# Latent attention's rotated keys on all 128 rows, with zeros in the other head's half

## The chip, the cores and the metric

One core of a Trainium2 chip runs the whole program. The time is device microseconds of one execution; the figure before is the median of three runs.

## What is computed

Two blocks on 256 tokens with 1024 features, all in float32: a retention layer and a latent-attention layer, each with a gated embedding behind it, then a block of convolution, pooling and a feed-forward part. The change concerns the scores of the latent attention, with 16 heads, of which this is the core:

```python
k_rope = rope(z[..., o2:o3][:, :, None, :], pos)[:, :, 0, :]
...
q = (c_q @ w_uq).reshape(B, S, MLA_HEADS, MLA_NOPE + MLA_ROPE)
q_nope = q[..., :MLA_NOPE]
q_rope = rope(q[..., MLA_NOPE:], pos)
q_abs = jnp.einsum('bshd,chd->bshc', q_nope, w_uk)
scale = (MLA_NOPE + MLA_ROPE) ** -0.5
q_cat = jnp.concatenate([q_abs, q_rope], axis=-1) * scale
k_cat = jnp.concatenate([c_kv, k_rope], axis=-1)
...
s = jnp.einsum('bqhc,bkc->bhqk', qb, k_cat).astype(jnp.float32)
s = jnp.where(key_idx[None, :] <= q_idx[:, None], s, neg)
pr = jax.nn.softmax(s, axis=-1).astype(c_kv.dtype)
```

A head's score is a sum of two products: one over 128 features without rotation, and one over 64 rotated features, whose keys all heads share.

## The kernel before

Activations lie transposed, features on the 128 rows and the 256 tokens along the columns. Weights come from DRAM in tiles of 128 x 1024, in the order of their use, through six buffers (`fetch`, L162). Each float32 operand of a product is taken as a sum of two parts, `hi` and `lo`, in the type float32r: ScalarE copies `hi` (L175 for weights, L184 for activations), VectorE subtracts for `lo` (L176, L185). `mm` (L233) then issues three products: hi x hi (L234), hi x lo (L235), lo x hi (L236). The profile calls a weight's parts `wh` and `wl`.

The order on TensorE is the order in which the program is written, with one device: `after(us, fn)` puts `fn` behind about so much emitted TensorE time. ScalarE, VectorE and GpSimd have their own queues, whose order the scheduler decides from the dependences.

In the retention layer, each of four heads multiplies keys with queries (L568), and values with scores (`ret_av`, L585 and L586: two values' blocks to a bank, two banks, each of 256 columns, then 128 more). Its rotary tables are `cosR` and `sinR` (L481, L482), last read at L555 and L556.

In the latent attention the heads go in pairs p = 0 to 7. The 64 rotated key features are computed twice over, so that rows 0 to 63 and rows 64 to 127 hold the same; `rope4` (L737) rotates them and splits them into `krh` and `krl`, once for all heads (L782). `mla_proj` (L823) makes a pair's queries: `qr` holds the rotated queries of head 2p on rows 0 to 63 and of head 2p + 1 on rows 64 to 127; `qn` and `kn` hold the 128 features without rotation. `mla_scores` (L852) takes, for each head e of the pair and each block of 128 queries, first the product over 128 rows (L861), then the one over the head's 64 rows (L862), both into the same sum:

```python
for e in range(2):
    pss = bank()
    rs = slice(64 * e, 64 * e + 64)
    for qb, (o, n) in enumerate(((0, P), (P, S))):
        qs = slice(qb * P, (qb + 1) * P)
        mm(pss[:, o:o + n], (qn[0][:, e, qs], qn[1][:, e, qs]), (kn[0][:, e, :n], kn[1][:, e, :n]), True, False)
        mm(pss[:, o:o + n], (qr[0][rs, qs], qr[1][rs, qs]), (kr[0][rs, :n], kr[1][rs, :n]), False, True)
```

That is 24 products to a pair: per head three of 128 columns on 128 rows, three of 128 on 64 rows, three of 256 on 128 rows, three of 256 on 64 rows. Here these 24 are called a score block; there are eight. Behind a block come the softmax on VectorE and ScalarE (L865 to L878), and on TensorE other work: gates (`mla_gate`, L800, whose product VectorE takes at L809) and the next pair's projections. `mla_turn` transposes the probabilities (L889), `mla_av` (L896) multiplies them with the values. Steps of the modulation (L409), a dot product per partition on VectorE of a tile that a transfer brings, are put between at a set rate.

Of the kernel before, what the change touches and what calls it, by code (L numbers as in the profile page):

```python
# [11 lines left out]
F32 = mybir.dt.float32  # L12
# [70 lines left out]
def tile_kernel(ctx, tc, order, xT, pT, pos, vec, cst, cv, wada, wts, outT):  # L83
# [22 lines left out]
    class Blk:  # L106
        """nb feature blocks of [128, 256], four to a tile."""
        def __init__(self, nb, dt=F32):
# [11 lines left out]
    class Wide(Blk):  # L120
        """eight blocks of 256 + extra columns"""
        def __init__(self, extra):
# [16 lines left out]

# [1 line left out]
    class Seq:  # L141
# [47 lines left out]

    # A start clears the accumulation bits of its whole PSUM bank, so a bank in which two  # L190
    # sums are open together is started once, over all its columns.
    def open_bank():
# [3 lines left out]

    # Emission order is the software pipeline: `after(us, fn)` emits fn once about that much
    # tensor-engine time has been emitted behind it, so that what fn waits for is done by then.
    clk = [0.0]
# [6 lines left out]

    # the modulation's steps on VectorE, one per `rate` of emitted tensor-engine time
    mods = {"rate": None, "last": 0.0, "n": 0}
# [36 lines left out]

# [1 line left out]
    xt = Blk(DB)  # L247
# [5 lines left out]

    # the first products are taken in float32, from the tiles as they come
    v0 = [("ret_in", kb * P, 2048) for kb in range(8)]
# [13 lines left out]
    V.memset(ones, 1.0)  # L269
    # the tensor engine's clock rises only after some microseconds of work: done while it waits  # L270
    wu = bank()
# [16 lines left out]

# [1 line left out]
    def sum_pairs(pairs):  # L290
        """squares of [128, 2, 256] pieces, added up"""
        tot = None
        for i, p in enumerate(pairs):
            sq = t2()
            A.activation(sq, p, AF.Square)
            if tot is None:
                tot = sq
            elif i < len(pairs) - 1:
                V.tensor_add(tot, tot, sq)
        return [tot, sq] if len(pairs) > 1 else [tot]  # L300

    def sum_ahead(pairs):
        """All but the last added up."""
        tot = pairs[0]
        for i, p in enumerate(pairs[1:-1]):
            new = t2() if i == 0 else tot
            V.tensor_add(new, tot, p)
            tot = new
        return [tot] + pairs[1:][-1:]

    def warm(x):
        """has the reciprocal square root's table loaded before it is waited for"""
        A.activation(small(1), x, AF.Abs_reciprocal_sqrt, bias=eps_r)

    class Sums:
        """Sums over the features of pieces [128, n, 256] that come one by one, and of their squares:
        the early pieces are added up, the last ones go to the tensor engine as they are."""
        def __init__(self, both, fold):
# [53 lines left out]
    def rms_neg2(ps, n, out=None):  # L372
        """-2/sqrt(sum/n + eps), on every partition."""
        ve = t1()
        V.tensor_scalar(ve, ps, 1.0 / n, RMS_EPS, MUL, ADD)
        r0 = t1()
        A.activation(r0, ps, AF.Abs_reciprocal_sqrt, bias=eps_r, scale=1.0 / n)
        return newton(r0, ve, t1(tag="nr", bufs=3) if out is None else out)

    def ln_stats(ps, n):  # L380
        """ps: sum, sum of squares -> mean, -2/sqrt(var + eps)."""
        mu = t1(tag="mu", bufs=2)
# [11 lines left out]

# [1 line left out]
    mod = cp.tile([P, 48], F32, name="mod")  # L396
# [22 lines left out]
    def every(us, n, step):  # L419
        """n calls of step, one per us of emitted tensor-engine time."""  # L420
        def run():
# [8 lines left out]

# [1 line left out]
    posf = t1(tag="posf", bufs=1)  # L432
# [29 lines left out]

    # =============== layer 0: retention ===============
    def prenorm(x, layer, then):
        """Split x*g; then(-2*rstd) once the sums are through."""
        pair = two(DB)
# [13 lines left out]

    cosR = cp.tile([P, S], F32, name="cosR")  # L481
    sinR = cp.tile([P, S], F32, name="sinR")  # L482
    rc = cp.tile([P, 2], F32, name="rc")
# [125 lines left out]

    # y = gated @ w_out, K = 2048, eight output tiles kept in four banks  # L610
    def out_proj(name, pairs, ka, rate, done, layer):
# [16 lines left out]
    class proj_banks:  # L628
        """eight tiles of output: three banks of two, and two of one"""
        def __init__(self):  # L630
# [8 lines left out]
        def piece(self, m):  # L639
            """the bank that tile m ends"""  # L640
            return self.b[m // 2] if m < 6 else self.b[m - 3][:, 0:1, :]

    def proj_sums(both, get, key):
        """what to do as tiles end: their sums, without the last two's wait for the others"""
        sums = Sums(both, {"r": 0, "m": 0, "d": 1}[key])
# [17 lines left out]
    def post(x, ys, sums, layer, prepared):  # L663
        """x + rms(y)*g, then the per-layer embedding gate."""
        x1 = Blk(DB)
# [24 lines left out]
    def half_outer(name, xpair, fin, nk=8):  # L690
        """x @ w, eight output tiles: the first four tiles k-outer, the rest n-outer."""
        seq = Seq([(name, kb * P, m * P) for kb in range(nk) for m in range(4)] + nouter(name, range(4, 8), range(nk)))
# [35 lines left out]

    # =============== layer 1: latent attention ===============
    gq = cp.tile([P, 8], F32, name="gq")  # L730
# [3 lines left out]
    krs = t1(tag="krs", bufs=1)  # L734
    kr = (cp.tile([P, S], F32R, name="krh"), cp.tile([P, S], F32R, name="krl"))

    def rope4(src, pair):  # L737
        """rows [x1, x2, x1, x2] x 32 -> rotated, split."""
        sw = t1()
# [5 lines left out]
        V.tensor_add(a, a, sw)  # L745
        split(pair[0], pair[1], a)

# [8 lines left out]
    def lora(banks, sq, n, first):  # L756
        """rms_norm of z = r*zr over n features, from the raw zr."""
        pst = bank()[:, :S]
# [22 lines left out]
    V.scalar_tensor_tensor(krs, pskr, -0.5, r1["nr"], MUL, MUL)  # L781
    rope4(krs, kr)  # L782
    sqkv = sum_pairs([pskv])
# [16 lines left out]
    def mla_gate(p):  # L800
        """silu gates of heads 2p, 2p + 1"""
        if p % 2 == 0:
# [20 lines left out]
    def mla_proj(p):  # L823
# [4 lines left out]
        qr = st["qr"] = (t1(F32R, "qrh", 2), t1(F32R, "qrl", 2))  # L828
        rope4(psr, qr)
        psq = bank2()  # L830
# [21 lines left out]
    def mla_scores(p):  # L852
# [3 lines left out]
        for e in range(2):  # L856
            pss = bank()
            rs = slice(64 * e, 64 * e + 64)
            for qb, (o, n) in enumerate(((0, P), (P, S))):
                qs = slice(qb * P, (qb + 1) * P)  # L860
                mm(pss[:, o:o + n], (qn[0][:, e, qs], qn[1][:, e, qs]), (kn[0][:, e, :n], kn[1][:, e, :n]), True, False)  # L861
                mm(pss[:, o:o + n], (qr[0][rs, qs], qr[1][rs, qs]), (kr[0][rs, :n], kr[1][rs, :n]), False, True)  # L862
            sm = tp.tile([P, 384], F32, tag="am", name=nm("sm"), bufs=2)
# [59 lines left out]

    # =============== block 2 ===============
    # modulation columns: sh1, sc1, g1, sh2, sc2, g2
    while mods["n"] < 41:
# [21 lines left out]
    def modulate(x, which, mu, nrl, pairs, pair, raw=None):  # L948
        """(x - mu) * rstd * (1 + scale) + shift, split."""
        shift = mod[:, 24 * which:24 * which + 8]  # L950
# [15 lines left out]

    # The first four tiles behind a layer norm are multiplied before its statistics are there:
    # the norm is linear in x but for a factor and an offset per token, which are applied to the
    # product, with the column vectors that the offsets need carried as extra moving columns.
    # These products are taken in float32, so that nothing has to be split for them.  # L970
    def ahead(extra):
# [6 lines left out]
    def ahead_mm(name, tiles, w, n, k_outer=4):  # L978
        """the first k_outer tiles side by side, the rest one after the other"""
        first, rest = tiles[:k_outer], tiles[k_outer:]  # L980
# [35 lines left out]
    def ahead_out(ps):  # L1016
        """-> value without its offset, offset column"""
        u = small(2)
# [21 lines left out]

    # one tap of two blocks: on VectorE alone, or with the products from ScalarE
    def conv_steps():
# [49 lines left out]

    # pooling
    # From here most tiles take their product in float32: one more pass, but no splitting on
    # VectorE, which the convolution needs.
    def in_tile(ps, m, parts):
# [175 lines left out]

    # the products of z*g*s with the two norms' factors and offsets put to them
    def up_ahead(i):
# [156 lines left out]
```

## Time and profile before

| | |
|---|---|
| median of three runs | 880.08 us (879.75 to 881.86) |
| span of the profiled execution, its own time on the page | 878.7 us |
| TensorE busy | 862.8 us (98%), 6472 products |
| loads of weights busy | 827.5 us (94%) |
| VectorE busy | 710.7 us (81%) |
| ScalarE busy | 558.0 us (64%) |
| GpSimd busy | 3.2 us |
| mean granted clock of TensorE | 0.989 |

The span runs from the first to the last instruction of one execution; the median of the runs lies 1.4 us above it. Products overlap in the records: one of 256 columns shows some 0.28 us, while the next one starts 0.12 us later. So a stretch of TensorE is read by the starts, not by adding up durations, and a busy share of 98% doesn't say how many products pass. The granted clock is given as a share of 2.4 GHz.

### The profile page before, as it was taken

How to read it: one execution, taken by the hardware profiler on the slowest of the kernel's cores; microseconds unless marked ns; L12 is line 12 of the kernel's file. 1: busy time of each engine (PE TensorE's matmuls, PEld its weight loads, DVE VectorE, ACT ScalarE, POOL GpSimd, SP SyncE). 2: the span in 40 equal slices, each digit the busy share in tenths (PEclk: the TensorE clock that was granted, in tenths of full speed). 3: DMA queues.
4: the chain of work that ended last, by engine and by line, in shares of the span. 5: the costliest groups of instructions: out<-in, count | busy, mean ns of one | idle time of the engine just before them, and what ended most of it. 6: DMA issues, size and time to landing. Idle time of an engine off the chain costs nothing.

```text
span 878.7 us, 16459 instructions
## 1 busy us (share of the span) xinstructions
PE 862.8 (98%) x6472; PEld 827.5 (94%) x6472; DVE 710.7 (81%) x1276; ACT 558.0 (64%) x942; POOL 3.2 (0%) x20
## 2 busy tenths in 40 slices
PE   8999999999999999999999999999999999999994
PEld 6989999999999999999999998999999999999993
DVE  6999778887878977698775578799677888889975
ACT  7666555545675786676554757999756676666533
POOL 0000000000000000000000000000000000000000
PEclk9999999999999999999999999999999999999997
DMA  8857566878466537265245444244464355567601
GB/s 332 320 199 249 186 230 203 280 261 304 147 211 206 229 123 257 103 218 189 98 133 168 169 173 161 99 167 170 144 223 137 132 189 188 188 227 255 204 35 48
DMA packets 46461, 165.95 MB, mean 189 GB/s; under 512 B 5168, under 2 KB 5936, under 8 KB 46384
## 3 DMA queue, kind: packets, MB, share of 16 engines
q1 hardware_dynamic: 46224, 164.39, 54.0%
q8 instruction: 50, 0.82, 0.4%
q0 software_dynamic: 160, 0.52, 0.2%
q14 instruction: 27, 0.22, 0.1%
HBM read 163.85 MB, written 1.05 MB: 188 GB/s over the span
## 4 chain that ended last, share of the span: by engine, by line
PE 97%; DVE 2%; DMA 1%; ACT 0%; SPq 0%; issue 0%
PE ps L234 28%; PE ps L235 27%; PE ps L236 27%; PE ps L240 9%; PE ps L359 2%; PE ps L337 1%; DMA half<-in_xT 1%; PE ps L889 1%; PE ps L194 1%; DVE t L1227 0%; DVE t L1224 0%; PE ps L1145 0%; PE ps L1137 0%; DVE half L676 0%; DVE wl L176 0%
## 5 line engine op out<-in xcount | busy, mean ns | idle before, releaser
L234 PE MATMUL ps<-half,wh 128*128 128x256 f32 x1680 | 476.7, 284 | 0.0
L235 PE MATMUL ps<-half,wh 128*128 128x256 f32 x1680 | 474.6, 283 | 0.1
L236 PE MATMUL ps<-half,wl 128*128 128x256 f32 x1680 | 472.5, 281 | 0.0
L175 ACT CAST wh<-raw 128x1024 fp32r<-128x1024 f32 x233 | 243.1, 1049 | 177.6 <-PE ps L235 132.5
L176 DVE TENSOR_TENSOR wl<-raw,wh 128x1024 fp32r<-128x1024 f32 x233 | 282.2, 1220 | 71.7 <-ACT wh L175 69.6
L235 PEld LDWEIGHTS ps<-half,wh 128*128 128x128 f32 x1680 | 318.1, 189 | 1.6 <-DVE half L185 0.7
L234 PEld LDWEIGHTS ps<-half,wh 128*128 128x128 f32 x1680 | 317.7, 189 | 1.6 <-issue 0.2
L236 PEld LDWEIGHTS ps<-half,wl 128*128 128x128 f32 x1680 | 318.6, 190 | 0.0
L240 PE MATMUL ps<-half,raw 128*128 128x256 f32 (+2 forms) x384 | 84.9, 380 | 0.0
L240 PEld LDWEIGHTS ps<-half,raw 128*128 128x128 f32 x384 | 72.5, 190 | 10.0
L409 DVE CUSTOM_DVE_ANT_0 adach<-adach,siluc 128x1024 f32<-128x1024 f32 x48 | 58.3, 1219 | 19.0 <-DMA adach<-in_wada 18.9
L1054 ACT ACTIVATE t<-apad,vec 128x256 f32<-128x256 f32 x106 | 44.4, 500 | 0.5 <-DVE half L1055 0.5
L1055 DVE TENSOR_TENSOR half<-half,t 128x512 f32<-128x512 f32 x53 | 36.4, 687 | 3.8 <-ACT t L1054 1.8
L184 ACT CAST half<-t 128x256 fp32r<-128x256 f32 (+1 forms) x47 | 20.6, 453 | 21.1 <-DVE t L1317 12.0
L234 PE MATMUL ps<-wh,half 128*128 128x512 f32 (+1 forms) x92 | 33.9, 370 | 0.0
L235 PE MATMUL ps<-wl,half 128*128 128x512 f32 (+1 forms) x92 | 32.7, 356 | 0.2 <-DVE wl L176 0.2
L236 PE MATMUL ps<-wh,half 128*128 128x512 f32 (+1 forms) x92 | 32.6, 355 | 0.0
L185 DVE TENSOR_TENSOR half<-t,half 128x256 fp32r<-128x256 f32 (+1 forms) x47 | 21.7, 483 | 3.7 <-ACT half L184 2.9
L1312 ACT ACTIVATE t<-ps,vec 128x256 f32<-128x256 f32 x38 | 21.0, 557 | 2.7 <-DVE t L1314 1.5
L235 PEld LDWEIGHTS ps<-wl,half 128*128 128x128 f32 x92 | 17.4, 189 | 2.9 <-DVE wl L176 0.6
L234 PEld LDWEIGHTS ps<-wh,half 128*128 128x128 f32 x92 | 17.4, 189 | 2.8 <-ACT wh L175 0.2
L236 PEld LDWEIGHTS ps<-wh,half 128*128 128x128 f32 x92 | 17.3, 188 | 2.6
(260 smaller groups left out, 997.4 us busy)
## 6 DMA issues: line engine op xcount, KB each, us to landing
raw<-in_wts SPq DMA_DIRECT2D x257, 512.0 KB, 4.1
adach<-in_wada SPq DMA_DIRECT2D x48, 512.0 KB, 4.5
half<-in_xT SPq DMA_DIRECT2D x4, 256.0 KB, 6.4
cst<-in_cst SPq DMA_DIRECT2D x1, 928.0 KB, 10.7
raw<-in_wts SPq DMA_DIRECT2D x2, 256.0 KB, 4.9
siluc<-in_cv SPq DMA_DIRECT2D x1, 512.0 KB, 8.8
t<-in_pT POOLq DMA_DIRECT2D x2, 256.0 KB, 4.6
out<-half SPq DMA_DIRECT2D x4, 128.0 KB, 2.0
```

What stands on the lines that cost most here:

```text
L175: A.copy(hi, raw)
L176: V.tensor_sub(lo, raw, hi.bitcast(F32))
L184: A.copy(hi, src)
L185: V.tensor_sub(lo, src, hi.bitcast(F32))
L234: T.matmul(ps, l[0], r[0], start=first, stop=False)
L235: T.matmul(ps, l[0], r[1], start=False, stop=False)
L236: T.matmul(ps, l[1], r[0], start=False, stop=last)
L240: T.matmul(ps, w, r, start=first, stop=last)
L409: V.tensor_tensor_reduce(ch, ch, sc, 1.0, 0.0, MUL, ADD, mod[:, n:n + 1])
L1054: A.activation(t[:, b, :], apad[:, i0 + b, k:k + S], AF.Copy, scale=w[b])
L1055: V.tensor_add(acc.pair(i0 // 2), acc.pair(i0 // 2), t)
L1312: A.activation(t[:, b, :], ps[:, b, :], AF.Identity, bias=col("b_dw_f_2", m), scale=w[2])
```

## The change

The keys are kept in two tiles instead of one, `kr[0]` for the first head of each pair and `kr[1]` for the second, each with both parts. In `kr[e]` the 64 rows of head e hold the rotated keys, the other 64 rows hold zeros. The second product of a score then runs over all 128 rows of `qr` and of `kr[e]`; the other head's queries meet the zeros.

The zeros are written by GpSimd, and the split into parts is done once for each half. `rope4` is given a function that takes the rotated tile, since only the keys are put down in this way; the queries are split as before. The two tiles lie in a pool of two buffers, tag `rot`, in which the retention's rotary tables `cosR` and `sinR` come to lie as well, in one tile.

```diff
-    cosR = cp.tile([P, S], F32, name="cosR")
-    sinR = cp.tile([P, S], F32, name="sinR")
+    rot = tp.tile([P, 2, S], F32, tag="rot", name="rot", bufs=2)
+    cosR, sinR = rot[:, 0, :], rot[:, 1, :]
...
-    kr = (cp.tile([P, S], F32R, name="krh"), cp.tile([P, S], F32R, name="krl"))
+    kr = [tp.tile([P, 2, S], F32R, tag="rot", name=nm("kr"), bufs=2) for _ in range(2)]
...
-    def rope4(src, pair):
+    def rope4(src, put):
...
-        split(pair[0], pair[1], a)
+        put(a)
+
+    def put_kr(a):
+        for e in range(2):
+            own, other = slice(64 * e, 64 * e + 64), slice(64 - 64 * e, 128 - 64 * e)
+            nc.gpsimd.memset(kr[e][other].bitcast(F32), 0.0)
+            split(kr[e][own, 0, :], kr[e][own, 1, :], a[own])
...
-    rope4(krs, kr)
+    rope4(krs, put_kr)
...
-        rope4(psr, qr)
+        rope4(psr, lambda a: split(qr[0], qr[1], a))
...
-            rs = slice(64 * e, 64 * e + 64)
             for qb, (o, n) in enumerate(((0, P), (P, S))):
                 qs = slice(qb * P, (qb + 1) * P)
                 mm(pss[:, o:o + n], (qn[0][:, e, qs], qn[1][:, e, qs]), (kn[0][:, e, :n], kn[1][:, e, :n]), True, False)
-                mm(pss[:, o:o + n], (qr[0][rs, qs], qr[1][rs, qs]), (kr[0][rs, :n], kr[1][rs, :n]), False, True)
+                mm(pss[:, o:o + n], (qr[0][:, qs], qr[1][:, qs]), (kr[e][:, 0, :n], kr[e][:, 1, :n]), False, True)
```

The rest of the diff takes comments out. TensorE and SyncE have the same instructions in the same order as before. On ScalarE the one split of the keys becomes two. Two places on other queues change.

VectorE, at the split of the rotated keys and the norm of the key latents behind it (L363 to L369 are the Newton step of a reciprocal root). Before:

```order
333 L185 TENSOR_TENSOR krl<-t_503_3059,krh 128x256
334 L363 TENSOR_TENSOR t_513_3103<-t_511_3100 128x256
335 L368 SCALAR_TENSOR_TENSOR t_514_3105<-t_510_3098,t_513_3103 128x256
336 L176 TENSOR_TENSOR wl_3293<-raw_3290,wh_3292 128x1024
337 L369 SCALAR_TENSOR_TENSOR t_512_3102<-t_514_3105,t_511_3100 128x256
```

and with the change:

```order
333 L185 TENSOR_TENSOR kr_2907<-t_505_3058,kr_2907 64x256
334 L185 TENSOR_TENSOR kr_2908<-t_505_3058,kr_2908 64x256
335 L363 TENSOR_TENSOR t_515_3106<-t_513_3103 128x256
336 L176 TENSOR_TENSOR wl_3296<-raw_3293,wh_3295 128x1024
337 L368 SCALAR_TENSOR_TENSOR t_516_3108<-t_512_3101,t_515_3106 128x256
```

The split of 128 rows has become two of 64, and the weight split behind it stands one place further ahead, before the second step of the norm. Some 15 rows on, a sum of squares (L299) likewise stands one place further ahead of a weight split.

GpSimd, from the program's beginning to the transfer of the first layer's embeddings (`in_pT`). Before:

```order
10 masks.py:199 ISA
11 masks.py:199 AFFINE_SELECT ident<-ident 128x128
12 L709 DMA t_393_2373<-in_pT 128x512
13 L1028 MEMSET apad 128x4x30
14 L709 DMA t_1035_5954<-in_pT 128x512
```

and with the change:

```order
10 masks.py:199 ISA
11 masks.py:199 AFFINE_SELECT ident<-ident 128x128
12 L752 MEMSET kr_2907 64x512
13 L752 MEMSET kr_2908 64x512
14 L709 DMA t_393_2372<-in_pT 128x512
15 L1034 MEMSET apad 128x4x30
```

The two clears stand ahead of that transfer's issue.

## Rows read from the trace of the kernel before

**Rows 1.** The chain of work that ended last, from the page, by engine.
```profile
PE 97%; DVE 2%; DMA 1%; ACT 0%; SPq 0%; issue 0%
```
**Rows 2.** Who waited for whom, TensorE, longest first: us in total, times, longest.
```profile
PE ps L240 <- DMA raw<-in_wts: 1.3, 1, 1.3
```
**Rows 3.** Timeline of TensorE, second score block: start us, us, engine, line, operation.
```profile
330.57 0.22 PE L234 MATMUL ps<-t,t 128*128 128x128 f32 x1
...
330.75 0.28 PE L236 MATMUL ps<-t,t 128*128 128x128 f32 x1
330.95 0.33 PE L234 MATMUL ps<-krh,t 64*128 64x128 f32 x1
...
334.59 0.39 PE L234 MATMUL ps<-half,wh 128*128 128x256 f32 x1
334.82 0.29 PE L235 MATMUL ps<-half,wh 128*128 128x256 f32 x1
```
**Rows 4.** Timeline of TensorE, retention's scores and values: first product, first behind the block.
```profile
89.27 0.28 PE L234 MATMUL ps<-ah,half 128*128 128x256 f32 x1
...
91.99 0.45 PE L234 MATMUL ps<-wh,half 128*128 128x512 f32 x1
```
**Rows 5.** Busy time by stretch: us, busy (count) by engine, PEclk, DMA share, GB/s.
```profile
10.00:302.00 292.00, 291.66 (x2213) 279.48 (x2212) 251.91 (x402) 177.09 (x242) 0.68 (x1) 1.00 0.68 238
306.54:309.95 3.41, 3.41 (x18) 3.41 (x18) 1.96 (x9) 0.06 (x1) 0.00 (x0) 0.50 0.28 108
310.00:361.00 51.00, 51.00 (x414) 49.48 (x414) 38.34 (x73) 37.51 (x61) 0.00 (x0) 1.00 0.52 180
361.17:364.57 3.40, 3.40 (x17) 3.17 (x16) 1.27 (x7) 0.12 (x2) 0.00 (x0) 0.50 0.19 76
364.60:419.00 54.40, 54.40 (x433) 51.92 (x431) 46.88 (x105) 38.86 (x76) 0.19 (x1) 1.00 0.55 192
419.19:422.59 3.40, 3.40 (x17) 3.40 (x17) 2.69 (x11) 1.09 (x5) 0.00 (x0) 0.50 0.05 16
422.60:868.00 445.40, 442.91 (x3320) 426.89 (x3319) 353.78 (x629) 292.45 (x540) 1.43 (x9) 1.00 0.47 160
```
**Rows 6.** The same by stretch, of instructions on the tile krh alone.
```profile
302.00:307.00 5.00, 2.33 (x8) 1.47 (x8) 0.00 (x0) 0.00 (x0) 0.95 0.92 350
357.00:362.00 5.00, 2.48 (x8) 1.52 (x8) 0.00 (x0) 0.00 (x0) 0.92 0.31 113
414.00:420.00 6.00, 2.33 (x8) 1.47 (x8) 0.00 (x0) 0.00 (x0) 0.93 0.69 242
```
**Rows 7.** Timeline of TensorE behind the first score block.
```profile
307.14 0.41 PE L235 MATMUL ps<-half,wh 128*128 128x256 f32 x1
307.35 0.41 PE L236 MATMUL ps<-half,wl 128*128 128x256 f32 x1
```
**Rows 8.** Timeline of VectorE behind the first score block, idle time in brackets.
```profile
306.20 1.22 DVE L409 CUSTOM_DVE_ANT_0 adach<-adach,siluc 128x1024 f32<-128x1024 f32 x1 [0.62 <-DMA adach<-in_wada]
...
308.42 0.08 DVE L866 DVE_READ_ACCUMULATOR2_ANT sm<- 128x1 f32 x1
310.26 0.69 DVE L809 SCALAR_TENSOR_TENSOR t<-ps,t 128x512 f32<-128x512 f32 x1 [1.75 <-PE ps L236]
...
311.27 1.23 DVE L176 TENSOR_TENSOR wl<-raw,wh 128x1024 fp32r<-128x1024 f32 x1 [0.24 <-ACT wh L175]
```
**Rows 9.** Timeline of TensorE, the first product that reads that weight split.
```profile
313.13 0.28 PE L236 MATMUL ps<-half,wl 128*128 128x256 f32 x1
```
**Rows 10.** The split of the keys (ScalarE): ns min/median/max, first and last start us.
```profile
L184 ACT CAST krh<-t x1: 388/388/388, 266.4 to 266.4; 128x256 fp32r<-128x256 f32 x1
```
**Rows 11.** The last reading of the rotary tables (VectorE), columns as above.
```profile
L556 DVE TENSOR_TENSOR t<-ps,sinR x8: 676/680/692, 31.5 to 154.4; 128x512 f32<-128x512 f32 x8
```
**Rows 12.** Timeline of GpSimd.
```profile
0.74 0.20 POOL masks.py:197 MEMSET ident<- 128x128 f32 x1 [0.29 <-POOLq L1414]
...
163.16 0.68 POOL L709 DMA_DIRECT2D t<-in_pT  x1 [161.73 <-PE ps L236]
```

## The prediction

> **What bounds the kernel now.** I read the chain of waits first: 97% of the span is TensorE's own work [rows 1]. Then the table of who waited for whom: the longest wait that TensorE has anywhere is 1.3 us, at the start, and none of its waits lies in the latent attention (258 to 484 us) [rows 2]. So TensorE is the bound, and a change there is worth what it takes off TensorE's own stream, as long as the operands keep up.
>
> Then the timeline of TensorE in one score block [rows 3]. It starts at 330.57 and the first product behind it at 334.59: 4.02 us for 24 products, twelve of 128 columns and twelve of 256. No wait is shown, but the pitch isn't even. From the third product on 128 rows (330.75) to the first on 64 rows (330.95) 0.20 us pass; at the way back, the first product behind the block takes 0.23 us until the next one (334.59 to 334.82). The ordinary pitch in this stage is 51.00 us for 414 products, 0.12 us [rows 5].
>
> For what the same mix costs on 128 rows all through there is a twin: the retention's product of scores and values, also 24 products, twelve of 128 columns and twelve of 256, with the operands changing tiles as here. It runs from 89.27 to 91.99, 2.72 us [rows 4].
>
> Last the granted clock by stretch [rows 5]. It is 1.00 from 10 us to 868 us, but for three stretches of 3.4 us at 0.50, that is at 1.2 instead of 2.4 GHz: from 306.54, 361.17 and 419.19. In each of the windows in which they begin lies a score block, by its products on 64 rows [rows 6]; the engine came straight out of the block each time. In such a stretch the pitch is 0.21 us [rows 7].
>
> **The change part by part.**
>
> *The products.* There are 8 score blocks, each with 12 products on 64 rows; number, columns and order of the products stay. A block alternates between 128 and 64 rows: four times down, and four times up with the step to what follows it. With all on 128 rows it should run like its twin: 4.02 - 2.72 = 1.30 us less, and the first product behind it takes 0.12 instead of 0.23 us, 0.11 less. 8 x 1.41 = **11.3 us**. Nothing hides this, since TensorE is the chain.
>
> A price that no row shows is that of these products with zeros in half of their rows. The nearest rows bound it: not under the twin's 2.72 us (the gain is at most 11.3), not over the block's 4.02 unless the loads of weights come out of hiding (a rival, below). I take the twin: same shapes, same pairs of split operands.
>
> The Trainium skill (TensorE: Matmul & The Clock Gate, Part 3: Packing small matmuls) says that a load of weights overlaps products in flight only where the row groups differ. By that, filling the rows up would put each load in line with its product, and the sum would be 6 us to the slow side. The trace speaks against it: the twin's 24 products on 128 rows, each with its own load, pass at 2.72 / 24 = 0.11 us [rows 4].
>
> *The clock.* A stretch at 0.50 costs the products that it doesn't do: 3.40 x (1 - 0.12 / 0.21) = 1.46 us. If the three falls come from the uneven blocks, all go: 3 x 1.46 = **4.4 us**. The bounds are nothing and this; for the full value speaks that every fall begins at a score block and none anywhere else in 858 us, the twin's four blocks with their 128-column products included.
>
> *What the gain leaves late.* Behind the first block VectorE isn't led by TensorE alone: at 306.20 it begins a modulation step that waited for a transfer, and is busy to 308.50 (308.42 and 0.08); the gate product that it takes at 310.26 was waited for 1.75 us [rows 8]. With block and fall gone (2.9 us) that product is there at 307.4, but VectorE takes it at 308.5. From there to its split of a weight tile it needs 311.27 - 310.26 less 0.24 idle, 0.77 us: the split runs 309.27 to 310.50. TensorE wants it 2.9 us before 313.13 [rows 9], at 310.2. That is a new wait of **0.3 us**. In the other blocks I found the operands with more room, and cost them at nothing; the cover is the time by which each split is ready before its use, 0.6 us at the least here (312.50 against 313.13).
>
> *The rotated keys.* The split of the keys, once, becomes two of 64 rows: one more instruction on ScalarE and one on VectorE, each at most what the 128-row one took, 0.39 us on ScalarE [rows 10], some 35 us before the first score block. On VectorE one weight split moves ahead of a step of the norm, by one place. I cost both at nothing: TensorE waits for nothing there; without that cover it would be 0.8 us.
>
> *The clears.* Two clears of 64 x 512 come onto GpSimd's queue, ahead of the transfer of the layer's embeddings. One needs the buffer of the retention's rotary tables, last read by VectorE at 154.4 plus 0.69 us [rows 11]; the transfer behind it is issued at 163.16 for another reason, a wait for TensorE [rows 12]. So 8 us are free. A clear of 128 x 128 took 0.20 us [rows 12]; by its columns, an estimate, one of 512 takes up to 0.8. Nothing is late.
>
> SyncE's queue and the order on TensorE stay as they are.
>
> **Sum.** -11.3 - 4.4 + 0.3 = -15.4 us. The profiled execution's span is 878.7, so 863.3; the median of the runs shown lies 1.4 above that span, and the same difference gives **864.7 us**.
>
> **The rivals.**
>
> *The clock still falls.* The falls may come from the 128-column products or from what stands behind the blocks, both of which stay. Against it: the twin has as many of them and no fall follows it. Then only the first term comes: 880.1 - 11.3 = 868.8.
>
> *The operands take over.* VectorE, ScalarE or a transfer don't move with TensorE, and what the blocks give up comes back as waits. For it: the 0.6 us of room behind the first block [rows 8, 9]. Against it: VectorE and ScalarE there wait for TensorE before their work (1.75 us), so most of the chain moves along. If none of it did behind the three blocks with a fall, 3 x (2.9 - 0.6) = 6.9 us come back: 871.6; half of it gives 868.
>
> *The rows aren't it.* The 0.20 us could belong to the step to another tile, and would stay: 880. Against it: the twin steps between tiles just so.
>
> *Slower.* The products on 128 rows can't hide their loads in this order, each costs as much as the one at the step does now, 0.20 us: 24 x 0.20 = 4.8 us a block instead of 4.02, 8 x 0.8 = 6.4 us more, 886.5. It decides where a block lasts over 4.02 us. The page's rule on row groups would have it so; the twin doesn't.
>
> **How the numbers follow.** Forecast 0.80 (its own range 862.5 to 866.5: four falls instead of three in the timed runs give 1.5 more, up to 2 us of waits take it back); falls stay 0.09; operands take over 0.07; rows aren't it 0.03; slower 0.01. The range reaches from 862.5 over the second case and half of the third to 869.3; outside lie the worst waits and the last two, with some room for what I haven't seen, 0.1 in all. About 0.3% (2.6 us) is what a measurement of this kernel can tell from no change. Faster by more than that: 0.80 + 0.09 + 0.07, less a little for a sum of small waits, 0.95; same 0.03; slower 0.02.
>
> **What would show it.** In the new profile each score block, from its first product to the first behind it, lasts 2.7 us with no pitch of 0.20 at the step to the rotated keys; the clock is 1.00 from 10 us to the last ten; TensorE's waits in the attention stay under 1 us in sum; the stages before 258 us take as long as now. Blocks of 2.7 us with falls behind them mean the first rival; new waits of TensorE for the splits or the softmax the second; blocks of 4 us the third; longer ones the last. If GpSimd's clears end after 163 us, or the span before 258 us grows, the step on the clears was wrong.

## The result and the profile after

The changed kernel takes 866.24 us (865.47 to 866.75, four runs) beside 880.97 us for the kernel before (four runs): a ratio of 0.9838, interval 0.9823 to 0.9853. The forecast was 864.7 us and 15.4 us less; 14.7 us less were measured. (The forecast set out from 880.08 us, the median of three runs; a fourth run raised it to 880.97.) The profiled execution has a span of 864.9 us.

The page of the kernel after; the chain row answers to [rows 1]:

```profile
PE 848.1 (98%) x6472; PEld 818.8 (95%) x6472; DVE 710.0 (82%) x1277; ACT 557.5 (64%) x943; POOL 4.2 (0%) x22
...
PE 95%; DVE 2%; DMA 2%; ACT 0%; issue 0%; SPq 0%; DVEq 0%
```

TensorE is still the chain. The timeline of TensorE in the second score block of the kernel after, beside [rows 3]: start us, us, engine, line, operation.

```profile
328.16 0.22 PE L234 MATMUL ps<-t,t 128*128 128x128 f32 x1
...
328.33 0.28 PE L236 MATMUL ps<-t,t 128*128 128x128 f32 x1
328.45 0.27 PE L234 MATMUL ps<-kr,t 128*128 128x128 f32 x1
...
330.93 0.28 PE L234 MATMUL ps<-half,wh 128*128 128x256 f32 x1
331.04 0.28 PE L235 MATMUL ps<-half,wh 128*128 128x256 f32 x1
```

The step to the rotated keys takes 0.12 us instead of 0.20, the product behind the block 0.11 instead of 0.23. The block lasts from 328.16 to 330.93, 2.77 us instead of 4.02.

Busy time and granted clock of the kernel after in one stretch from the start-up to the last ten us, beside [rows 5]: us, busy (count) by engine, PEclk, DMA share, GB/s.

```profile
11.50:854.00 842.50, 838.49 (x6447) 812.74 (x6446) 699.32 (x1244) 548.84 (x928) 2.83 (x12) 1.00 0.57 192
```

The granted clock is 1.00 all through; the three stretches at 0.50 are gone. Two views of what is new: who waited for whom on TensorE over the whole span, longest first (us in total, times, longest), and the timeline of TensorE at the second pair's transposes.

```profile
PE ps L273 <- DVE eps_l L277: 1.1, 1, 1.1
PE ps L895 <- DVE sm L884: 1.0, 1, 1.0
PE ps L337 <- DVE t L346: 0.9, 1, 0.9
PE ps L240 <- DMA raw<-in_wts: 0.8, 1, 0.8
PE ps L235 <- DVE wl L176: 0.5, 1, 0.5
```

```profile
339.43 0.49 PE L895 MATMUL ps<-ident,sm 128*128 128x128 f32 x3
340.94 0.61 PE L895 MATMUL ps<-ident,sm 128*128 128x128 f32 x3 [1.01 <-DVE sm L884]
```

L895 are the transposes of the probabilities. TensorE waits 1.0 us for the softmax of the pair's second head; before, that wait wasn't there. What VectorE did until then, from its timeline:

```profile
334.63 1.22 DVE L409 CUSTOM_DVE_ANT_0 adach<-adach,siluc 128x1024 f32<-128x1024 f32 x1 [3.44 <-DMA adach<-in_wada]
...
339.36 1.23 DVE L409 CUSTOM_DVE_ANT_0 adach<-adach,siluc 128x1024 f32<-128x1024 f32 x1 [0.52 <-DMA adach<-in_wada]
340.51 0.55 DVE L884 TENSOR_SCALAR sm<-sm,sm 128x128 f32<-128x128 f32 x2
```

The same two steps in the kernel before:

```profile
336.62 1.22 DVE L409 CUSTOM_DVE_ANT_0 adach<-adach,siluc 128x1024 f32<-128x1024 f32 x1 [2.91 <-DMA adach<-in_wada]
...
340.75 1.21 DVE L409 CUSTOM_DVE_ANT_0 adach<-adach,siluc 128x1024 f32<-128x1024 f32 x1
```

Two modulation steps (L409) stand in VectorE's queue among the softmax steps, and each waits for its transfer, 3.44 and 0.52 us, with the softmax behind it. Before, the second didn't wait. The two transfers are issued 2.5 us earlier than before, but the two steps start only 2.0 and 1.4 us earlier, while TensorE is 3.8 us ahead behind this block. The transfers move along with TensorE in part only.

GpSimd's two clears, from its timeline, beside [rows 12]:

```profile
1.49 0.52 POOL L752 MEMSET kr<- 64x512 f32 x1
155.53 0.52 POOL L752 MEMSET kr<- 64x512 f32 x1 [153.51 <-DVE t L556]
163.50 0.68 POOL L709 DMA_DIRECT2D t<-in_pT  x1 [7.45 <-PE ps L236]
```

The second waits for the last reading of the rotary tables, and the transfer behind it still waits 7.45 us for TensorE.

### The profile page after: what moved, and what is told of

Read it like the earlier page. It is cut to its first block, busy times and chain, and to the rows that moved or that the text cites. A ratio compares the mean times of both kernels' runs of the same rounds, so it can differ in the third digit from the quotient of the medians.

```text
span 864.9 us, 16461 instructions
## 1 busy us (share of the span) xinstructions
PE 848.1 (98%) x6472; PEld 818.8 (95%) x6472; DVE 710.0 (82%) x1277; ACT 557.5 (64%) x943; POOL 4.2 (0%) x22
## 4 chain that ended last, share of the span: by engine, by line
PE 95%; DVE 2%; DMA 2%; ACT 0%; issue 0%; SPq 0%; DVEq 0%
PE ps L235 27%; PE ps L234 27%; PE ps L236 27%; PE ps L240 10%; PE ps L359 2%; PE ps L337 1%; DMA adach<-in_wada 1%; DMA half<-in_xT 1%; PE ps L895 1%; PE ps L194 1%; DVE wl L176 0%; DVE t L1233 0%; DVE t L1230 0%; PE ps L1143 0%; PE ps L1151 0%
## 5 line engine op out<-in xcount | busy, mean ns | idle before, releaser
L409 DVE CUSTOM_DVE_ANT_0 adach<-adach,siluc 128x1024 f32<-128x1024 f32 x48 | 58.5, 1222 | 18.1 <-DMA adach<-in_wada 18.1
```

Of the source, the lines that this page charges most:

```text
L409: V.tensor_tensor_reduce(ch, ch, sc, 1.0, 0.0, MUL, ADD, mod[:, n:n + 1])
```

## The experiments

My theory: the time went into the steps between products on 128 and on 64 rows, and into the falls of the clock that the blocks full of such steps brought. The rivals: something else of the change brought the gain; products on 64 rows are slow wherever they stand; the clock falls because half of the rows idle. In the code cuts, `...` stands for lines that are left out.

**The rows alone back (rows64).**

```diff
+                rs = slice(64 * e, 64 * e + 64)
-                mm(pss[:, o:o + n], (qr[0][:, qs], qr[1][:, qs]), (kr[e][:, 0, :n], kr[e][:, 1, :n]), False, True)
+                mm(pss[:, o:o + n], (qr[0][rs, qs], qr[1][rs, qs]), (kr[e][rs, 0, :n], kr[e][rs, 1, :n]), False, True)
```

> The changed kernel, its tiles, clears and two half splits kept, but each score's second product again reads only the head's 64 rows of them. If the step between 128 and 64 rows is what cost the time: score blocks of 4.02 us again, two to four falls of the granted clock behind them, 880 to 881 us. If anything else of the change (where the keys lie, the split by halves) brought the gain: blocks of 2.8 us and 866 us.

Measured: 880.39 us, ratio to the kernel before 0.9994 (0.9970 to 1.0018). All is lost again with this one edit: tiles, clears and half splits bring and cost nothing that can be measured. Seven blocks of its profile last 3.99 to 4.00 us. One thing came out otherwise: there is one fall of the clock in its profile and not two to four, and it begins in the eighth block; busy time by stretch:

```profile
447.90:454.60 6.70, 6.70 (x30) 6.48 (x31) 4.04 (x14) 2.48 (x8) 0.54 (x1) 0.50 0.26 97
```

It lasts 6.7 us, as long as two of those in [rows 5]. So how many falls there are differs between executions of all but the same products. The ten runs lie between 877.4 and 885.2 us, those of the changed kernel within 1.3 us. No profile was kept of the other runs, but the mean granted clock of each run is on record, and it goes with the time: 0.993 in the run of 877.44 us, 0.984 in that of 885.19; 0.994 to 0.996 in the changed kernel's four. A fall of 3.4 us lowers the mean by 0.002; so, an estimate, those 0.009 are four to five falls, or some 7 us at the prediction's price, of the 7.75 between the two runs.

**Half of the steps (half64).**

```diff
+                rs = slice(64 * e, 128)
-                mm(pss[:, o:o + n], (qr[0][:, qs], qr[1][:, qs]), (kr[e][:, 0, :n], kr[e][:, 1, :n]), False, True)
+                mm(pss[:, o:o + n], (qr[0][rs, qs], qr[1][rs, qs]), (kr[e][rs, 0, :n], kr[e][rs, 1, :n]), False, True)
```

> The changed kernel with only the second head of each pair back on 64 rows: four steps between row counts to a block instead of eight or none. If the cost goes by steps, at 0.18 us each (1.36 us of the block and 0.11 behind it, over eight): blocks of 3.4 us, 866 + 8 x 0.7 = 872 us without falls of the clock. If the clock falls by the whole block's unevenness, none or one fall; if any product on 64 rows can bring it, up to three, 876 us.

Measured: 870.53 us, ratio 0.9879 (0.9847 to 0.9911). Its second block, from the timeline of TensorE:

```profile
328.33 0.23 PE L234 MATMUL ps<-t,t 128*128 128x128 f32 x1
...
331.66 0.39 PE L234 MATMUL ps<-half,wh 128*128 128x256 f32 x1
331.88 0.28 PE L235 MATMUL ps<-half,wh 128*128 128x256 f32 x1
```

3.33 us a block: 0.56 over the changed kernel's, with 0.11 more behind it 0.67 for four steps, 0.17 us each. The 0.18 that I had expected counts the 0.11 behind the block twice. No fall of the clock. Eight blocks of that give 5.4 us; 4.3 us are the difference of the medians. The rest is the new wait of the changed kernel, which this one doesn't have: TensorE waits for nothing between 300 and 450 us.

**Three times the steps (alternate).** The kernel before, its products in turn:

```diff
-                mm(pss[:, o:o + n], (qn[0][:, e, qs], qn[1][:, e, qs]), (kn[0][:, e, :n], kn[1][:, e, :n]), True, False)
-                mm(pss[:, o:o + n], (qr[0][rs, qs], qr[1][rs, qs]), (kr[0][rs, :n], kr[1][rs, :n]), False, True)
+                two_l = (qn[0][:, e, qs], qn[1][:, e, qs]), (qr[0][rs, qs], qr[1][rs, qs])
+                two_r = (kn[0][:, e, :n], kn[1][:, e, :n]), (kr[0][rs, :n], kr[1][rs, :n])
+                for j, (x, y) in enumerate(((0, 0), (0, 1), (1, 0))):
+                    for f in range(2):
+                        T.matmul(pss[:, o:o + n], two_l[f][x], two_r[f][y], start=j + f == 0, stop=j + f == 3)
...
```

> The kernel before, with the same 24 products to a block in another order: one on 128 rows, one on 64, and so on, so that there are 24 steps between row counts instead of eight. If the step costs, 0.18 us each: blocks of 2.76 + 24 x 0.18 = 7 us, so 866 + 8 x 4.3 = 901 us, and with a fall of the clock behind each block 913 or more. If it is the product on 64 rows that is slow, wherever it stands: blocks of 4 us and 880 us as before.

Measured: 924.84 us, ratio 1.0493 (1.0450 to 1.0537). The number and the kind of the products are the same as before; only their order is another. From the timeline of TensorE in its first block:

```profile
301.72 0.22 PE L865 MATMUL ps<-t,t 128*128 128x128 f32 x1
301.87 0.32 PE L865 MATMUL ps<-krh,t 64*128 64x128 f32 x1
302.12 0.33 PE L865 MATMUL ps<-t,t 128*128 128x128 f32 x1
302.38 0.33 PE L865 MATMUL ps<-krl,t 64*128 64x128 f32 x1
...
305.02 0.33 PE L865 MATMUL ps<-t,t 128*128 128x128 f32 x1
```

From the second product on, the pitch is 0.25 to 0.26 us at each product of 128 columns, on 128 and on 64 rows alike. The first half of the block, still at the full clock, takes 3.30 us for twelve steps (301.72 to 305.02); half of the changed kernel's block is 1.38, so a step costs 0.16 us here. So it is the step, not the product on 64 rows. The clock falls at every one of the eight blocks; the first fall lasts 10 us and begins inside the block (301.72 to 310.35):

```profile
305.30:315.40 10.10, 10.10 (x35) 8.18 (x35) 3.73 (x16) 1.96 (x5) 0.00 (x0) 0.50 0.10 38
```

The eight last 68 us together. The falls were longer than I expected, which is why the time lies above the 913 us.

**No product of a block on 128 rows (all64).** As rows64, and the first product too, on the head's rows alone:

```diff
-                mm(pss[:, o:o + n], (qn[0][:, e, qs], qn[1][:, e, qs]), (kn[0][:, e, :n], kn[1][:, e, :n]), True, False)
+                mm(pss[:, o:o + n], (qn[0][rs, e, qs], qn[1][rs, e, qs]), (kn[0][rs, e, :n], kn[1][rs, e, :n]), True, False)
```

> The changed kernel with all 24 products of a block on the head's 64 rows; the other half of the features without rotation is left out of the scores. Steps: down at the block's start, from the first head's rows to the second's in its middle, up at its end. If only the step costs: blocks of 2.9 to 3.2 us, 867 to 870 us, no falls. If products on 64 rows are slow in themselves: blocks over 4.5 us. If the clock falls because half of the rows idle, not because of the steps: falls behind most of the eight blocks, at 1.5 us each, 875 us or more.

This kernel leaves out half of the features without rotation. Measured: 866.07 us (one run), blocks of 2.58 us, no fall. That is less than the changed kernel's 2.77 us, in spite of the steps at both ends. The timeline of TensorE in the middle of the first block shows why:

```profile
303.18 0.28 PE L236 MATMUL ps<-t,t 64*128 64x256 f32 x1
303.18 0.32 PE L234 MATMUL ps<-t,t 64*128 64x128 f32 x1
303.29 0.27 PE L234 MATMUL ps<-kr,t 64*128 64x256 f32 x1
303.35 0.27 PE L235 MATMUL ps<-t,t 64*128 64x128 f32 x1
303.41 0.28 PE L235 MATMUL ps<-kr,t 64*128 64x256 f32 x1
303.46 0.27 PE L236 MATMUL ps<-t,t 64*128 64x128 f32 x1
```

The products of 128 columns are the second head's, on rows 64 to 127; they run between those of the first head, on rows 0 to 63, though they stand behind all of them in the program. So neither half-used rows nor the products on 64 rows make a block slow, and eight blocks on half of the rows brought no fall of the clock. That half-used rows never do isn't shown, since the two heads also overlapped and it is one run.

**Side by side on purpose (pair4, pairz).** If products on different rows pass together, the zeros could be spared. pair4 is the kernel before in this order:

```diff
+        banks = [bank(), bank()]
+        for qb, (o, n) in enumerate(((0, P), (P, S))):
+            qs = slice(qb * P, (qb + 1) * P)
+            for e in range(2):
+                mm(banks[e][:, o:o + n], (qn[0][:, e, qs], qn[1][:, e, qs]), (kn[0][:, e, :n], kn[1][:, e, :n]), True, False)
+            for j, (x, y) in enumerate(((0, 0), (0, 1), (1, 0))):
+                for e in range(2):
+                    rs = slice(64 * e, 64 * e + 64)
+                    T.matmul(banks[e][:, o:o + n], qr[x][rs, qs], kr[y][rs, :n], start=False, stop=j == 2)
...
```

> The kernel before, without zeros, its 24 products to a block in another order: both heads' products on 128 rows for the first queries, then the two heads' products on 64 rows in turn, one on rows 0 to 63 and one on 64 to 127, then the same for the second queries. Four steps between row counts. If two products on different rows run side by side (in the run with all products on 64 rows the second head's started 7 ns behind one of the first): 12 x 0.113 + 6 x 0.115 + 4 x 0.18 = 2.8 us a block, 866 us, no gain over the zeros. If they don't: 2.76 + 4 x 0.18 = 3.5 us, 872 us. If each change of rows is a step: 16 of them, 5.6 us, 889 us or more.

Measured: 872.18 us, ratio 0.9908 (0.9878 to 0.9937). From its timeline of TensorE (x2 are the two heads' products, 2 to 9 ns apart), and its waits on TensorE from 300 to 450 us:

```profile
302.34 0.22 PE L234 MATMUL ps<-t,t 128*128 128x128 f32 x1
...
303.05 0.33 PE L864 MATMUL ps<-krh,t 64*128 64x128 f32 x2
303.22 0.28 PE L864 MATMUL ps<-krl,t 64*128 64x128 f32 x2
303.33 0.27 PE L864 MATMUL ps<-krh,t 64*128 64x128 f32 x2
...
304.97 0.39 PE L234 MATMUL ps<-half,wh 128*128 128x256 f32 x1
```

```profile
PE ps L895 <- DVE sm L884: 4.2, 3, 1.9
PE ps L236 <- DVE wl L176: 0.9, 2, 0.7
```

The products do pass side by side, and the block is 2.63 us long, shorter than with zeros. Yet the kernel is 6 us slower. It took the 872 us that I had set for products not side by side, but not for that reason: TensorE waits 4.2 us instead of 1.0 for the softmax, and 0.9 for weight splits. That is 4.1 of the 5.1 us between the spans (870.0 and 864.9); the rest isn't traced. In this order the first head's scores are whole only at the end of the block, not in its middle, and VectorE takes a modulation step ahead of their softmax (L871), from its timeline behind the first block:

```profile
306.51 1.22 DVE L409 CUSTOM_DVE_ANT_0 adach<-adach,siluc 128x1024 f32<-128x1024 f32 x1 [1.45 <-DMA adach<-in_wada]
...
307.66 0.28 DVE L871 CUSTOM_DVE_ANT_0 sm<-ps,cst 128x128 f32<-128x128 f32 x1
```

In the changed kernel that softmax begins at 304.94 us, before the step. How much of the waits comes from the order of the products and how much from the step isn't shown. pairz takes all twelve products on 128 rows first:

> As the run before it, but with all twelve products on 128 rows first and all twelve on 64 rows behind them, so that two steps are left; for this each of the two banks is opened by a product with zeros over 384 columns, 0.16 us each. Side by side: 0.32 + 1.36 + 0.69 + 0.36 = 2.7 us a block, 866 us, even with the zeros in the keys. Not side by side: 3.4 us, 871 us.

Measured: 870.66 us, ratio 0.9874 (0.9839 to 0.9909; one of its four runs took 4787.78 us, for no reason that the record shows, and isn't in the ratio): side by side again, 2.70 us a block, with 2.4 us of waits at the transposes and 1.0 for weight splits. Again that is near the 871 us that I had set for products not side by side, and again there are new waits instead. Both say the same: what is left here isn't TensorE's alone.

**The new wait (turn_late, ada_later).** First the transposes of the second pair are put back:

```diff
-        after(7.6, lambda: mla_turn(p))
+        after(8.8 if p == 1 else 7.6, lambda: mla_turn(p))
```

> The changed kernel with the second pair's transposes put 1.2 us further back in TensorE's order; in the changed kernel TensorE waits there 1.0 us for the softmax, behind a modulation step whose transfer doesn't move with TensorE. If that wait is a loss that room undoes: it falls to under 0.1 us, 865.2 us. If the delay only moves it on (the products of values behind it, the buffers): a wait of about as much elsewhere in the same stage, 866 us.

Measured: 866.23 us, ratio 0.9832 (0.9808 to 0.9855), no difference to the changed kernel. The wait at the transposes is gone, and one stands at the second product of the third block instead:

```profile
PE ps L235 <- DVE t L185: 0.5, 1, 0.5
```

Between the first and the second product of that block 0.74 us pass, where it was 0.06. Then the modulation step is put off instead:

```diff
+        if p == 1:
+            mods["last"] = clk[0]
         after(7.6, lambda: mla_turn(p))
```

> The changed kernel with the modulation step that stands between the second pair's softmax steps on VectorE put off by one turn, the transposes where they were. If the 1.0 us for which TensorE waits at those transposes comes from that step, whose transfer lands by its own time: the wait goes, 865.2 us. If the softmax is late by itself, by ScalarE or by TensorE having got faster: the wait stays at about 1 us, 866.2 us. If the wait goes and another of its size comes further on, as with the transposes put back: 866.2 us too.

Measured: 865.35 us, ratio 0.9835 (0.9810 to 0.9860). In its profile TensorE waits for nothing between 300 and 450 us, and the eighth block starts 1.1 us earlier than in the changed kernel's profile; so the step was the cause of that wait. Its median is the lowest of all kernels here, 0.9 us under the changed kernel's; the intervals overlap, so that it is faster isn't shown.

## Why the prediction was right

*The first term, 11.3 us.* The eight blocks sum to 32.25 us in the trace before and to 22.08 in the one after, 10.2 us; with 0.11 us behind each it is 11.1. The twin was the right price to 0.05 us a block: 2.76 in place of 2.72, since the twin's first product of 256 columns doesn't follow one of 128: it passes in 0.12 us, the three that do in 0.17. That the step is the cause is shown by half64 and alternate: the cost goes with the number of steps (none, 4, 8: blocks of 2.77, 3.33, 4.01 us; 24: 3.30 us for the first half of a block), and rows64 shows that nothing else of the change matters.

*The second term, 4.4 us.* No fall is left, so in this pair of profiles it came in full. It is less firm than the first: the profile of rows64 had one fall of 6.7 us where that of the kernel before had three of 3.4, so what the term is worth varies by execution. In thirteen later runs of the kernel before the mean granted clock went from 0.992 to 0.984, against 0.995 in the changed kernel's profile: by the 0.002 a fall, an estimate, two to six falls. That the one profile read ahead of the forecast held three, near the middle, is luck. One reading was off too: the engine hadn't come out of the third block when its fall began, at 361.17; that block ended at 361.52. No kernel with four steps or fewer to a block showed a fall in the attention in its profile, that with 24 showed one at each. So the falls go with the number of steps; what it is in such blocks that the clock answers to isn't shown.

*The wait, 0.3 us.* Here the step was placed wrongly. The weight split behind the first block ran from 309.27 us, at the time that I had worked out, but TensorE had started the whole attention 0.36 us later than before (first block at 302.64, not 302.28) and didn't wait. That is the spread between executions: turn_late, the same program up to there, starts that block at 302.33 us. It didn't wait either, for its modulation step began at 305.28 us and not at 306.37. So whether this wait comes hangs on when the transfer lands. The wait of 1.0 us came behind the second block, one of those whose operands I had found "with more room" and "cost them at nothing". The same pattern, a modulation step whose transfer moves with TensorE only in part, stands there too, and there it is the transposes that wait. I had followed the pattern behind one block and not behind the others. The sign that I had set, waits under 1 us in sum, is just missed.

*The things costed at nothing* were nothing: the clears took 0.52 us each and left the transfer 7.45 us of waiting to spare; no wait stands at the key split.

*The sum.* By TensorE's starts the wait costs 1.2 us, 1.0 of it shown as idle time. -11.1 - 4.3 (a little of the third block's fall lies in the blocks) + 1.2 + 0.4 at the start: -13.8, and the spans differ by 13.8. The forecast for the span, 863.3, was 1.6 us low: 0.9 from the wait, 0.4 from the start, 0.2 from the blocks, 0.1 from the falls.

*The rivals.* The clock's, the rows' and the slower one fell; of the operands', which put up to 6.9 us on new waits, 1.2 us came. In the new blocks products on 128 rows, each with a load of its own, pass with a pitch of 0.11 to 0.12 us. The rule of the Trainium skill (TensorE: Matmul & The Clock Gate, Part 3: Packing small matmuls), that a load is hidden only beside products on other rows, would put loads and products in line; it doesn't hold here. What the same section of the Trainium skill says of products on different rows, that they run side by side, agrees with the 2 to 9 ns between the starts in pair4.

## What to carry to other kernels

Where products with a short contraction stand among full ones, look at the starts of TensorE's products and not at its busy share: 98% busy hid 11 us. Filling the rows with zeros costs a clear and takes the step away; if the short products are left, gather them, since each step costs and no single product on 64 rows did here. And when the bounding engine gets faster, go through each place where a queue holds work that waits for a transfer: such work moves along only in part (2.0 and 1.4 us of 3.8 here), and what stands behind it can become the next wait.

## What I hadn't expected of the hardware

A step between 128 and 64 rows, down or up, cost 0.16 to 0.17 us in these blocks, though TensorE's record shows no idle time. Products on rows 0 to 63 and on rows 64 to 127 that are written one right behind the other started 2 to 9 ns apart in pair4, and in all64 products started before earlier ones on the other rows (303.18 and 303.29 us). The clock fell to half while TensorE's records show it busy without a gap, for 3.4 us in the kernel before, 6.7 us in rows64 and up to 10 us in alternate.
